# A two-layer model block with product-key experts: its second layer, second block and retrieval run for half the tokens at a time, and two token tiles are gathered instead of one

## The chip, the cores and the metric

The kernel runs on one core of a Trainium2 chip. The time is device microseconds (us) of one execution. A core has TensorE (PE, with its weight loads PEld), VectorE (DVE), ScalarE (ACT), GpSimd (POOL) and SyncE (SP), which issues most of the DMAs. All matrices are f32; a product of full accuracy is made either directly in f32, which the trace shows as two records per matmul, or in three passes of the rounded type fp32r.

## The reference

512 tokens of width 1024, with 16 meta tokens ahead of them, go through a first block of two layers, a second block, and a layer of product-key experts. Cut to what matters:

```python
for l in range(2):                                 # first block
    xn = _rmsnorm(h, pre_norm_g[l])
    proj = xn @ w_in[l] + b_in[l]                  # ten parts, 10240 columns
    y_a = _short_conv_branch(...)                  # looks back two tokens
    y_b = _retention_branch(...)                   # a token sees those before it
    y = (sigmoid(g_a) * y_a + sigmoid(g_b) * y_b) @ w_o[l]
    h = h + _rmsnorm(y, post_norm_g[l])
xn = rms_norm(h, norm1_g)                          # second block
h = h + concat(hgrn2(xn), gla(xn)) @ w_out         # two gated linear attentions, causal
hn = rms_norm(h, norm2_g)
q = (hn @ w_q).reshape(tokens, 8, 2, 128)          # retrieval: 8 heads, 2 x 128 sub-keys
s_top, i_top = top_k(q . sub_keys, 16)             # then the best 16 of the 256 sums
expert, g = ..., softmax(best)                     # 128 experts for each token, of 16384
act = gelu(einsum('td,thkd->thk', hn, u[expert]))
h = h + einsum('thk,thkd->td', g * act, v[expert])
return rms_norm(h, norm_f_g)
```

Every layer and the second block look back only: the first 256 tokens never need the last 256.

## The kernel before, in words

**Weights.** All weights, U and V among them, lie in one DRAM array `ws`, cut in pieces of 128 x 1024. The program is a list of tasks, each with the pieces that it uses. `Weights.run` goes through it: it loads pieces in pairs of 1 MB, issued by SP (`raw`); it splits a piece into `hi` (ScalarE, L143) and `lo` = raw - hi (VectorE, L151), two pieces ahead and at high priority; then it calls the task, which makes three passes (hi.hi, lo.hi, hi.lo; L386, L887, L1721, L1765). A task with `direct=True` takes the raw piece in f32 (L688, L1718).

**Tokens.** The moving operand holds tokens as columns. Layer 0 and layer 1 run for all tokens: each weight is used for a first part of 272 or 256 columns and a second of 256. The second block and the retrieval have the two halves as separate steps, whose order `PLAN` writes out (the first digit of a word is the half): FQ, KG, V and G are products with weights, S scores, M the mix, O the output, N the norm ahead of the retrieval, Q the retrieval's queries and keys.

**Background work.** Generators given to `W.later` or `bg` (norms, scores, `top_k`, the gate matrix) are advanced by `W.pace` steps per piece, from `PACE`; `W.flush` runs them out at once. A tile scheduler then sets each engine's order; every engine runs its instructions in that order.

**Experts.** Of four tiles of 128 tokens, the first three (`NDENSE`, ND = 384 columns) go through all 16384 experts densely: `gate_matrix` makes a dense matrix of the weights of the retrieved experts (L1438 and L1445 on VectorE, L1453 on TensorE) and puts it into DRAM as `gate_d`; `u_task` makes 128 experts' activations (the first `AHEAD` = 28 of the 128 groups direct, L1718, the rest L1721), `weigh` multiplies them by the gates (L1738) and splits them (`hw`, L203, L204), and `v_task` (L1765) sums V over them in PSUM. The fourth tile is gathered: for each of its 128 slots `fetch` brings one row of U and V for each token, 8 KB, by an indirect DMA that GpSimd issues (L1635) into one of four buffers; VectorE makes the dot product (L1671) and the weighted sum (L1663). The gather runs in the background of the dense stage, from expert group 6 on.

## Time and profile before

| what | value |
|---|---|
| median of 3 runs | 3297.1 us (3294.66 to 3298.0) |
| the profiled execution | 3293.4 us, its span 3291.6 |
| TensorE matmul, busy | 3250.3 us, 99% of the span |
| VectorE, busy | 2036.7 us, 62% |
| ScalarE, busy | 1302.2 us, 40% |
| GpSimd, busy | 186.3 us, 6% |
| DMA | 532 MB, mean 162 GB/s |

The span is the time from the first to the last instruction that the profiler recorded. Busy time is that of instructions on the engine; a wait isn't busy. The engines run beside each other, so the shares don't add up to one.

### The profile page before, as it was taken

The numbers are of one execution on the slowest core, as the hardware profiler recorded it, in microseconds if no ns is written. First come the engines' busy times: TensorE is split into PE (matmuls) and PEld (weight loads), VectorE is DVE, ScalarE is ACT, GpSimd is POOL, SyncE is SP. The second block draws the span as 40 slices with busy tenths as digits, with TensorE's granted clock in tenths as the row PEclk, the third lists the DMA queues.
The fourth block names the chain that finished last, engine by engine and source line by source line (L and its number), as shares of the span: only waits on it lengthen the run. The fifth ranks groups of instructions, "written<-read, shape, count | busy, mean of one in ns | idle before, by whom it ended". The sixth has DMA issues, their size and how long they took to land. (4 is left out here: it accounts for less than half of the span.)

```text
span 3291.6 us, 51099 instructions
## 1 busy us (share of the span) xinstructions
PE 3250.3 (99%) x21063; PEld 2974.2 (90%) x21063; DVE 2036.7 (62%) x4019; ACT 1302.2 (40%) x2388; POOL 186.3 (6%) x132
## 2 busy tenths in 40 slices
PE   8999999999999999999999999999999999999999
PEld 7999999999889999999998988766789999999998
DVE  6545554433744555443465659998898888888443
ACT  5343242323534324232455533356443333333333
POOL 0000000000000000000000000000132222222000
PEclk9999999999999999999999999999999999999999
DMA  6222222222422222222232123346899988998442
GB/s 216 75 86 88 77 78 90 90 90 103 176 75 99 87 84 78 90 90 100 106 129 90 52 91 140 129 181 239 305 373 346 345 333 314 351 356 325 143 147 95
DMA packets 129961, 532.04 MB, mean 162 GB/s; under 512 B 9136, under 2 KB 60992, under 8 KB 73280
## 3 DMA queue, kind: packets, MB, share of 16 engines
q1 hardware_dynamic: 103520, 368.19, 31.2%
q0 software_dynamic: 18432, 134.23, 10.6%
q10 hardware_dynamic: 7776, 26.37, 2.0%
q8 instruction: 165, 2.70, 0.3%
q14 instruction: 68, 0.56, 0.0%
HBM read 501.48 MB, written 27.26 MB: 161 GB/s over the span
## 5 line engine op out<-in xcount | busy, mean ns | idle before, releaser
L143 ACT ACTIVATE hi<-raw 128x1024 fp32r<-128x1024 f32 x532 | 563.4, 1060 | 1404.1 <-PE ps L386 626.7
L151 DVE TENSOR_TENSOR lo<-raw,hi 128x1024 fp32r<-128x1024 f32 x532 | 650.6, 1224 | 753.3 <-ACT hi L143 748.4
L386 PE MATMUL ps<-xnh,hi 128*128 128x256 f32 (+1 forms) x2464 | 513.7, 283 | 0.0
L386 PE MATMUL ps<-xnl,hi 128*128 128x256 f32 (+1 forms) x2464 | 513.5, 283 | 0.0
L386 PE MATMUL ps<-xnh,lo 128*128 128x256 f32 (+1 forms) x2464 | 512.9, 283 | 0.0
L1765 PE MATMUL ps<-hi,hw 128*128 128x512 f32 x1536 | 427.0, 393 | 3.3 <-ACT hid L1730 2.8
L1721 PE MATMUL ps<-hn,hi 128*128 128x384 f32 x1600 | 409.5, 337 | 0.0
L386 PEld LDWEIGHTS ps<-xnh,lo 128*128 128x128 f32 x2464 | 385.8, 189 | 0.0
L386 PEld LDWEIGHTS ps<-xnh,hi 128*128 128x128 f32 x2464 | 384.7, 188 | 1.1
L386 PEld LDWEIGHTS ps<-xnl,hi 128*128 128x128 f32 x2464 | 384.4, 188 | 0.1
L1635 POOL DMA_INDIRECT uv<-uv,idx x128 | 186.1, 1454 | 2843.8 <-PE ps L1650 2336.8
L1765 PEld LDWEIGHTS ps<-hi,hw 128*128 128x128 f32 x1536 | 287.7, 188 | 63.6 <-ACT hid L1730 3.5
L1721 PEld LDWEIGHTS ps<-hn,hi 128*128 128x128 f32 x1600 | 290.8, 188 | 4.3
L1721 PE MATMUL ps<-hn,lo 128*128 128x384 f32 x800 | 269.2, 337 | 0.0
L1765 PE MATMUL ps<-lo,hw 128*128 128x512 f32 x768 | 239.5, 392 | 0.0
L1765 PEld LDWEIGHTS ps<-lo,hw 128*128 128x128 f32 x768 | 144.7, 188 | 32.1
L1663 DVE SCALAR_TENSOR_TENSOR acc<-uv,dots,acc 128x1024 f32<-128x1024 f32 x127 | 163.0, 1284 | 3.2
L1671 DVE SCALAR_TENSOR_TENSOR uv<-uv,hnT 128x1024 f32<-128x1024 f32 x128 | 155.8, 1219 | 10.5 <-DMA uv<-uv,idx 10.4
L1718 PE MATMUL ps<-hn,raw 128*128 128x384 f32 x448 | 149.5, 490 | 5.0 <-ACT stage L1462 4.7
L1721 PEld LDWEIGHTS ps<-hn,lo 128*128 128x128 f32 x800 | 150.0, 188 | 0.1
L887 PE MATMUL ps<-x,hi 128*128 128x256 f32 x768 | 141.4, 288 | 4.0 <-ACT x L274 3.4
L1718 PEld LDWEIGHTS ps<-hn,raw 128*128 128x128 f32 x448 | 83.4, 190 | 62.6 <-ACT stage L1462 8.1
(353 smaller groups left out, 5103.6 us busy)
## 6 DMA issues: line engine op xcount, KB each, us to landing
raw<-ws SPq DMA_DIRECT2D x313, 1024.0 KB, 4.8
gate_d<-stage ACTq DMA_DIRECT2D x48, 512.0 KB, 3.4
gates<-gate_d SPq DMA_DIRECT2D x16, 1536.0 KB, 13.1
dm<-decay_m SPq DMA_DIRECT2D x8, 264.0 KB, 5.1
vb<-vbias SPq DMA_DIRECT2D x8, 256.0 KB, 6.3
dc<-decay SPq DMA_DIRECT2D x8, 256.0 KB, 5.6
uv<-uv,idx POOLq DMA_INDIRECT x128, 7.6
h<-ht SPq DMA_DIRECT2D x2, 544.0 KB, 4.4
```

Source lines behind the costliest of these rows:

```text
L143: nc.scalar.activation(hi, raw[i], AF.Copy)
L151: nc.vector.tensor_tensor(out=lo, in0=r, in1=parts[i][0].bitcast(F32), op=OP.subtract)
L386: nc.tensor.matmul(t[:, :b - a], w[wi][:, off + k, :], x[k].t[xi][:, a:b], start=(k == 0 and n == 0), stop=(k == K - 1 and n == 2))
L887: nc.tensor.matmul(p, parts[wi][:, k, :], x[k][:, xi], start=(k == 0 and n == 0), stop=(k == K - 1 and n == 2))
L1635: nc.gpsimd.indirect_dma_start(out=t, out_offset=None, in_=ins["uv"], in_offset=bass.IndirectOffsetOnAxis(ap=idx[i][:, j:j + 1], axis=0))
L1663: nc.vector.scalar_tensor_tensor(out=acc, in0=v, scalar=dots[:, j:j + 1], in1=acc, op0=OP.mult, op1=OP.add)
L1671: nc.vector.scalar_tensor_tensor(out=u, in0=u, scalar=1.0, in1=hnT, op0=OP.mult, op1=OP.mult, accum_out=dots[:, j:j + 1])
L1718: nc.tensor.matmul(ps, w[0][:, k, :], tl["hn32"][k][:, :ND], start=k == 0, stop=k == KD - 1)
L1721: nc.tensor.matmul(ps, w[wi][:, k, :], tl["hn"][k][:, xi], start=(k == 0 and n == 0), stop=(k == KD - 1 and n == 2))
L1765: mm = nc.tensor.matmul(tl["acc"][t][b], h[:, hi, t * 128:(t + 1) * 128], w[vi][:, b * 512:(b + 1) * 512], start=(e == 0 and n == 0), stop ...
```

## The change

Layer 0 stays as it was. What follows is done for the first 256 tokens (with the meta tokens) up to and including the retrieval's queries, then for the other 256: layer 1 (`late_layer`, called by `second_layer`), the second block by a shorter `PLAN`, the retrieval. All pieces of layer 1, the second block and the retrieval's queries are read, and where it applies split, once for each half. What the second half needs of the first (keys and values of both blocks) goes to DRAM and is read back (`left_kq`, `left_vm`, `left_vh`, `left_k`, `left_v`).

Tiles 0 and 1 are now gathered, tiles 2 and 3 dense (ND = 256, the first 32 groups of U direct). U and V rows are gathered apart, 256 rows of 4 KB for each token, into three buffers (`ROWS`). The generator of the gather has a queue of its own, `W.slow`, advanced by `pace2` steps per piece: 1.45 from the retrieval of tiles 0 and 1 on, 1.1 in the dense stage; `end_gathering` runs it out at expert group 124. From piece 128 on (layer 1 and everything behind it), `lo` of every second piece is made by GpSimd. The output projection of layer 1 and the second block's FQ are direct for both halves. Line numbers of the changed kernel: L812 and L806 are passes and direct products of layer 1, L1337 the second block's direct ones, L158 `lo`, L2085 the dot product, L2096 the weighted sum, L1871 and L1878 the gate matrix, L2141 the product with the gates, L211 the split's second part.

```diff
-NDENSE = 3
-ND = 128 * NDENSE
-NHN = 3
-AHEAD = 22 + 2 * NHN
-PACE = (3, 1, 2, 2, 2, 3.75, 6.5, 1.5, 1, 0.7)
+ND = HALF
+AHEAD = 32
+PACE = (3, 1, 2, 2, 2, 3.75, 6.5, 1.5)
+GATHER = (1.45, 1.1)
+ROWS = 3
+POOLED = 128
 SAFTER = 1
-QCUT = 15
 TICK2, TICKU = 4, 2
...
-PLAN = "FQ00 P3 S00 P4 FQ01 S01 !N1 KG V0 G0 FQ10 S02 V1 S10 M00 FQ11 S11 G1 S12 M01 M10 O0 P8 M11 N0 Q00 O1 Q01 N1 P5 Q1"
+PLAN = "FQ0 P3 S0 P4 FQ1 S1 KG S2 V0 G0 V1 F G1 M0 M1 O N Q"
...
         self.pump(int(self.credit))
         self.credit -= int(self.credit)
+        self.credit2 = min(self.credit2 + self.pace2 * share, 3)
+        while self.credit2 >= 1 and self.slow:
+            self.credit2 -= 1
+            if next(self.slow[0], self) is self:
+                self.slow.pop(0)
...
-                    nc.vector.tensor_tensor(out=lo, in0=r, in1=parts[i][0].bitcast(F32), op=OP.subtract)
+                    eng = nc.gpsimd if flat[i][0] >= POOLED and i % 2 else nc.vector
+                    eng.tensor_tensor(out=lo, in0=r, in1=parts[i][0].bitcast(F32), op=OP.subtract)
...
+                def wo_task(m):
+                    def f(w):
+                        if m % 2 == 0:
+                            st["y2", m // 2] = slot("y2", 2 * N).rearrange("p (a c) -> p a c", a=2)
+                        ps = proj(w, 0, N, x=[st["yb", k // 2][:, k % 2] for k in range(KD)])
+                        y = st["y2", m // 2][:, m % 2]
+                        nc.scalar.activation(y, ps, AF.Copy)
+                        st.setdefault("ss", Sum()).add(y)
+                    return f
...
+                def post_norm():
+                    r = rstd_of(slot("rstd", N), st["ss"].total())
+                    yield
+                    total = Sum()
+                    for m in range(KD):
+                        x = hs[m][:, q0:f1]
+                        y = st["y2", m // 2][:, m % 2]
+                        nc.vector.scalar_tensor_tensor(out=y, in0=y, scalar=col(C_POST + m), in1=r,
+                                                       op0=OP.mult, op1=OP.mult)
+                        nc.vector.tensor_tensor(out=x, in0=x, in1=y, op=OP.add)
+                        total.add(x)
...
+            def second_norms(half):
+                total = yield from late[half]["post_norm"]()
+                yield from halves[half]["norm1"](total)
...
+            def second_layer(half):
...
+                    for m in range(KD):
+                        add(L["wo_task"](m), direct=True)
...
+                do(W.flush)
+                if half == 0:
+                    do(phase, 1)
+                    bg(first_norms, 1)
+                do(setattr, W, "pace", PACE[0])
+                order(L, 1, add, qk, wo)
...
+                            W.add(H["pair_task"](which, 2 * a + c), N0 + 4 * a + 2 * k + c, direct=True)
...
+                    do(lambda: W.later(H["norm2"](), name="norm2", first=True))
                     do(W.flush, "norm2")
...
+                    do(H["load_keys"])
+                    if s == 0:
+                        do(lambda: W.later(first_block.late[1]["pre_norm"](rstd2[:, HALF:]), first=True))
+                    for c in range(16):
+                        W.add(H["wq_task"](c), N0 + 36 + c, direct=s == 1)
+                    do(H["keys"], 15)
+                    if s == 0:
+                        do(lambda: W.later(experts.begin(), name="top0"))
+            for s in range(2):
+                first_block.second_layer(s)
+                bg(first_block.second_norms, s)
+                do(W.flush)
+                for word in PLAN.split():
+                    if word[0] == "P":
+                        do(setattr, W, "pace", PACE[int(word[1:])])
+                    else:
+                        name = word.rstrip("01234")
+                        step(s, name, int(word[len(name):] or 0))
...
+        def begin():
+            gp = ctx.enter_context(tc.tile_pool(name="gather", bufs=1, side="right", reuse_waits="tile"))
+            W.slow.extend(gathered(i, gp) for i in range(2))
+            W.pace2 = GATHER[0]
+            yield
...
+            def row():
+                return p.tile([128, D], F32, tag="row", bufs=ROWS, name="row")
...
+                if j < 2 * NSLOT:
+                    t = rows[j] = row()
+                    table, j = ("pu", j) if j < NSLOT else ("pv", j - NSLOT)
...
+            dots = p.tile([128, NSLOT], F32, tag="dots", name="dots")
+            acc = p.tile([128, D], F32, tag="acc", name="acc")
+            for j in range(NSLOT):
+                u = rows.pop(j)
+                nc.vector.scalar_tensor_tensor(out=u, in0=u, scalar=1.0, in1=hnT, op0=OP.mult,
+                                               op1=OP.mult, accum_out=dots[:, j:j + 1])
+                fetch(j + ROWS)
+                yield
+            nc.scalar.activation(dots, dots, AF.Gelu)
+            nc.vector.tensor_tensor(out=dots, in0=dots, in1=gw[i], op=OP.mult)
+            for j in range(NSLOT):
+                v = rows.pop(NSLOT + j)
+                if j == 0:
+                    nc.vector.tensor_scalar(out=acc, in0=v, scalar1=dots[:, j:j + 1], scalar2=None, op0=OP.mult)
+                else:
+                    nc.vector.scalar_tensor_tensor(out=acc, in0=v, scalar=dots[:, j:j + 1], in1=acc,
+                                                   op0=OP.mult, op1=OP.add)
+                fetch(NSLOT + j + ROWS)
+                yield
...
+        def end_gathering():
+            for x in W.slow:
+                for _ in x:
+                    pass
+            W.slow.clear()
-        for e in (*range(18, AHEAD), *range(18)):
+        for e in range(AHEAD):
             if e == 8:
-                do(W.flush, "top")
+                do(W.flush, "top1")
...
+        do(setattr, W, "pace2", GATHER[1])
         for e in range(0, 128, 2):
-            if e == ENDS:
-                do(W.flush)
+            if e == 124:
+                do(end_gathering)
```

Where layer 1 ends and the second block begins, TensorE of the kernel before has (`yc` a branch of layer 1, `sg` the operand of its output projection, `sq` the squares of a norm, `nt` the normed tokens):

```order
L688 MATMUL ps<-sg,raw 128x256 x8
L247 MATMUL ps<-sq,mean 128x256
L688 MATMUL ps<-sg,raw 128x256 x32
L247 MATMUL ps<-sq,mean 128x256
L688 MATMUL ps<-sg,raw 128x256 x24
L883 MATMUL ps<-nt,raw 128x256 x15
L247 MATMUL ps<-sq,mean 128x256
L883 MATMUL ps<-nt,raw 128x256 x33
```

and the changed kernel, at the end of each half's layer 1 (L254 the norms' sums, L1680 the low gate):

```order
L812 MATMUL ps<-yc,hi 128x256 x2
L812 MATMUL ps<-yc,lo 128x256
L806 MATMUL ps<-yb,raw 128x256 x63
L254 MATMUL ps<-sq,mean 128x256 x2
L1337 MATMUL ps<-nt,raw 128x256 x6
L1680 MATMUL ps<-x,glp 16x256
L1337 MATMUL ps<-nt,raw 128x256 x40
```

Before, the norms' sums stood among the matmuls of the output projection and of FQ; now two stand together between them.

In the stage of the direct U, VectorE before has the gate matrix alone (`oh` the one-hot rows of 4 tokens):

```order
L1445 TENSOR_TENSOR oh<-oh,picks_102 128x1024 x2
L1438 TENSOR_TENSOR oh<-it_100,picks_102 128x1024 x2
L1445 TENSOR_TENSOR oh<-oh,picks_102 128x1024 x2
L1438 TENSOR_TENSOR oh<-it_100,picks_102 128x1024 x2
L1445 TENSOR_TENSOR oh<-oh,picks_102 128x1024 x2
```

and the changed kernel there:

```order
L1871 TENSOR_TENSOR oh<-it_97,picks_100 128x1024 x2
L1878 TENSOR_TENSOR oh<-oh,picks_100 128x1024 x2
L2085 SCALAR_TENSOR_TENSOR row,dots<-row,hnT 128x1024
L1871 TENSOR_TENSOR oh<-it_97,picks_100 128x1024 x2
L2085 SCALAR_TENSOR_TENSOR row,dots<-row,hnT 128x1024 x2
L1878 TENSOR_TENSOR oh<-oh,picks_100 128x1024 x2
L1871 TENSOR_TENSOR oh<-it_97,picks_100 128x1024 x2
L1878 TENSOR_TENSOR oh<-oh,picks_100 128x1024 x2
L1871 TENSOR_TENSOR oh<-it_97,picks_100 128x1024 x2
L2085 SCALAR_TENSOR_TENSOR row,dots<-row,hnT 128x1024
```

Dot products of gathered rows have moved in among the gate matrix.

At the end of the program VectorE before has the last products with the gates, the last splits, and the final norm (L1612, L1623):

```order
L1738 TENSOR_TENSOR hid<-hid,gates 128x384
L204 TENSOR_TENSOR hw<-hid,hw 128x384
L151 TENSOR_TENSOR lo<-raw,hi 128x1024
L204 TENSOR_TENSOR hw<-hid,hw 128x384
L1612 TENSOR_TENSOR r<-ss 128x1
L1623 SCALAR_TENSOR_TENSOR o<-ps,r,gf 128x512 x2
```

and the changed kernel (L2106 adds the residual to the gathered tile):

```order
L2096 SCALAR_TENSOR_TENSOR acc<-row,dots,acc 128x1024
L158 TENSOR_TENSOR lo<-raw,hi 128x1024
L2141 TENSOR_TENSOR early<-early,gates 128x256
L2096 SCALAR_TENSOR_TENSOR acc<-row,dots,acc 128x1024
L211 TENSOR_TENSOR hw<-early,hw 128x256
L2096 SCALAR_TENSOR_TENSOR acc<-row,dots,acc 128x1024 x35
L2106 TENSOR_TENSOR acc<-ps,acc 128x512 x2
```

Behind the last split now stand 35 weighted sums of the gather and the end of its tile.

## Rows read from the trace of the kernel before

**Rows 1.** The page, busy time, share of the span and instructions of each engine.

```profile
PE 3250.3 (99%) x21063; PEld 2974.2 (90%) x21063; DVE 2036.7 (62%) x4019; ACT 1302.2 (40%) x2388; POOL 186.3 (6%) x132
```

**Rows 2.** Windows by stage: us, busy of PE, PEld, DVE, ACT, POOL, PEclk, DMA, GB/s.

```profile
12.50:846.00 833.50, 833.50 (x6098) 798.39 (x6099) 410.47 (x678) 303.50 (x530) 0.00 (x0) 1.00 0.27 97
846.00:1660.00 814.00, 814.00 (x6026) 778.44 (x6025) 395.16 (x621) 296.62 (x507) 0.00 (x0) 1.00 0.28 98
1660.00:2113.00 453.00, 444.06 (x2945) 403.98 (x2944) 320.23 (x1114) 214.62 (x457) 0.00 (x0) 0.98 0.29 103
2113.00:2323.00 210.00, 197.55 (x1226) 131.17 (x1224) 181.69 (x553) 125.05 (x273) 0.00 (x0) 1.00 0.55 205
2323.00:3291.60 968.60, 958.63 (x4770) 861.14 (x4768) 724.30 (x1040) 357.35 (x613) 186.09 (x128) 1.00 0.77 286
```

**Rows 3.** Windows of one line's matmuls: L386, L688, L1721, L1765 (us, PE, PEld).

```profile
1500.00:1600.00 100.00, 100.00 (x848) 100.00 (x847) 1.00 0.27 96
...
1631.40:1660.00 28.60, 27.93 (x128) 24.24 (x128) 1.00 0.31 111
...
2323.00:3291.60 968.60, 429.03 (x2400) 421.98 (x2400) 1.00 0.77 286
...
2323.00:3291.60 968.60, 540.43 (x2304) 432.40 (x2304) 1.00 0.77 286
```

**Rows 4.** Groups of instructions: busy us, mean ns of one, idle before and its releaser.

```profile
L1453 PE MATMUL ps<-oh 128*128 128x128 f16 x768 | 51.4, 219 | 7.4 <-ACT stage L1462 5.6 <-DVE oh L1438 1.5 <-DVE oh L1445 0.3
...
L143 ACT ACTIVATE hi<-raw 128x1024 fp32r<-128x1024 f32 x532 | 563.4, 1060 | 1404.1 <-PE ps L386 626.7
...
L1671 DVE SCALAR_TENSOR_TENSOR uv<-uv,hnT 128x1024 f32<-128x1024 f32 x128 | 155.8, 1219 | 10.5 <-DMA uv<-uv,idx 10.4
...
L1671 DVE DVE_READ_ACCUMULATOR uv<-uv,hnT 128x1 f32 x128 | 10.6, 83 | 0.0
...
L1663 DVE SCALAR_TENSOR_TENSOR acc<-uv,dots,acc 128x1024 f32<-128x1024 f32 x127 | 163.0, 1284 | 3.2
...
L1438 DVE TENSOR_TENSOR oh<-it,picks 128x1024 f16<-128x1024 f16 x96 | 63.0, 686 | 22.4 <-PE ps L1453 22.1
L1445 DVE TENSOR_TENSOR oh<-oh,picks 128x1024 f16<-128x1024 f16 x96 | 61.9, 684 | 0.0
...
L204 DVE TENSOR_TENSOR hw<-hid,hw 128x384 fp32r<-128x384 f32 x128 | 70.7, 553 | 5.4 <-ACT hw L203 5.4
...
L151 DVE TENSOR_TENSOR lo<-raw,hi 128x1024 fp32r<-128x1024 f32 x532 | 650.6, 1224 | 753.3 <-ACT hi L143 748.4
```

**Rows 5.** Windows, a stretch of the dense stage; the last column is GB/s.

```profile
2340.00:2500.00 160.00, 159.52 (x738) 135.99 (x737) 141.45 (x209) 61.89 (x109) 47.44 (x31) 1.00 0.97 365
```

**Rows 6.** The window of both retrievals; a top-k step on VectorE there and up to 2323.

```profile
1958.00:2113.00 155.00, 150.67 (x906) 138.84 (x907) 139.55 (x758) 58.20 (x142) 0.00 (x0) 0.96 0.36 130
...
L1322 DVE MAX8 best<-cand 128x8 f32<-128x88 f32 x22 | 5.0, 246 | 0.0
...
L1322 DVE MAX8 best<-cand 128x8 f32<-128x88 f32 x10 | 2.0, 236 | 0.0
```

**Rows 7.** The window of the second block, both halves.

```profile
1660.00:1958.00 298.00, 293.38 (x2039) 265.14 (x2037) 180.68 (x357) 156.42 (x316) 0.00 (x0) 1.00 0.25 89
```

**Rows 8.** A group of the post-norm on VectorE.

```profile
L703 DVE SCALAR_TENSOR_TENSOR y<-y,cols,rstd 128x256 f32<-128x256 f32 (+1 forms) x32 | 13.2, 483 | 8.8 <-ACT rstd L249 8.8
```

**Rows 9.** Waits of TensorE: what for, us in total, times, longest.

```profile
PE ps L247 <- DVE sq L353: 8.3, 2, 7.2
...
PE ps L887 <- ACT x L274: 3.4, 1, 3.4
```

**Rows 10.** GpSimd's group; one record's min/median/max in ns; the gather's DMA to landing.

```profile
L1635 POOL DMA_INDIRECT uv<-uv,idx x128 | 186.1, 1454 | 2843.8 <-PE ps L1650 2336.8 <-DVE acc L1663 480.0 <-DVE acc L1661 15.1
...
L1635 POOL DMA_INDIRECT uv<-uv,idx x128: 939/1678/2752, 2337.3 to 3028.7; - x128
...
DMA to landing us min/median/max: 5.5/7.6/14.4
```

More of the change, by code (lines that the diff above doesn't have):

```diff
@@ L711, in first_block @@
                 layers.append(layer)
[L713 to L734 removed]
+            cols1 = []
@@ L799, in first_block @@
                         add(L["g_task"](m + 2, "b"))
-                    if m == KD - 3:
+                    if m == KD - 3 and l == 0:
                         do(L["halve_all"])
-                at = n[0]
-                if l == 1:
-                    do(lambda: second_block.tables())
-                for half in range(2):
-                    if half:
-                        if l == 0:
-                            do(layers[1]["setup"])
-                        do(setattr, W, "pace", PACE[2])
-                        bg(norm_between, l, 0)
-                    n[0] = at
-                    for m in range(KD):
-                        add(L["wo_task"](m, *OWN[l][half]), direct=half == 1)
@@ new lines, in first_layer, with add, qk, wo @@
+            def first_layer():
+                L = layers[0]
+                n = [0]
+                def add(f, **k):
+                    W.add(f, n[0], **k)
+                    n[0] += 1
+                def qk(h):
+                    for half in range(2) if h == 0 else [None]:
+                        if h == 0:
+                            n[0] = 0
+                        for hh in (0, 1) if h == 0 else [h]:
+                            for which in "qk":
+                                for part in range(2):
+                                    rng = FULL if half is None else [FULL[half]]
+                                    add(L["qk_task"](hh, which, part, rng),
+                                        direct=half == 0 and 4 * hh + 2 * "qk".index(which) + part < DIRECT[0])
+                        if half == 0:
+                            do(W.flush)
+                def wo():
+                    at = n[0]
+                    do(end_beside)
+                    do(late_setup)
+                    for half in range(2):
+                        if half:
+                            do(setattr, W, "pace", PACE[2])
+                            bg(first_norms, 0)
+                        n[0] = at
+                        for m in range(KD):
+                            add(L["wo_task"](m, *FULL[half]), direct=half == 1)
+                    assert n[0] == 128
+                do(L["setup"])
+                bg(L["pre_norm"], *FULL[0])
+                do(W.flush)
+                bg(L["pre_norm"], *FULL[1])
+                do(setattr, W, "pace", PACE[0])
+                order(L, 0, add, qk, wo)
@@ new lines, in second_layer, with add, qk, wo @@
+            def second_layer(half):
+                L = late[half]
+                n = [128]
+                def add(f, **k):
+                    W.add(f, n[0], **k)
+                    n[0] += 1
+                def qk(h):
+                    for hh in (0, 1) if h == 0 else [h]:
+                        for which in "qk":
+                            for part in range(2):
+                                add(L["qk_task"](hh, which, part),
+                                    direct=half == 0 and 4 * hh + 2 * "qk".index(which) + part < DIRECT[1])
+                def wo():
+                    do(second_block.tables if half == 0 else (lambda: None))
+                    for m in range(KD):
+                        add(L["wo_task"](m), direct=True)
+                    assert n[0] == 256
+                do(W.flush)
+                if half == 0:
+                    do(phase, 1)
+                    bg(first_norms, 1)
+                do(setattr, W, "pace", PACE[0])
+                order(L, 1, add, qk, wo)
@@ L1757, in f @@
                 prev = None
[L1758 removed]
+                for t in range(2):
                     one = [(e, h, w) for e, h, w in zip(es, hw, ws)]
```

785 lines of the change are left out of this document (504 added, 281 removed).

## The prediction

> **What bounds the kernel now.** I read the page's busy times first, then the span cut into stages, then the groups of the stages that change, then the waits of TensorE. The matmul engine is busy for 99% of the span [rows 1]: time is saved where its work shrinks, and lost where the change makes it wait. The sum is made against the profiled execution, 3293.4 us (the span of 3291.6 and 1.8 around it), which lies 3.7 under the median of the runs shown, 3297.1. A change of under 0.2%, some 7 us, can't be told from none.
>
> The stages [rows 2] are, in turn: layer 0, layer 1, second block with both retrievals, gate matrix with the direct part of U, dense experts. In each of them TensorE is busy for 94 to 100% of the time. The other columns show who has room. VectorE is busy half the time in the layers, 71% in the third, 87% in the fourth (181.7 of 210.0), 75% in the fifth. In the fifth the DMA engines run at 286 GB/s, and GpSimd does nothing but issue the gather.
>
> **What TensorE no longer does.** A matmul takes its time by its columns [rows 3]: with 256 columns 100.0/848 = 0.118 us in three passes, and 27.93/128 = 0.218 for one of the two records of a direct one; with 384 columns 429.0/2400 = 0.179 in passes; V's with 512 columns 540.4/2304 = 0.235.
> - Dense stage. U goes to 96 experts x 24 = 2304 matmuls of 256 columns, 272 us; V to 128 x 12 = 1536, 360 us. With 10 for the residual and the end it is 642 in place of 968.6: **-327**.
> - Direct U: 32 experts x 16 records x 0.218 = 112. The gate matrix took 51.4 [rows 4] for three tiles, so 34 for two. Together 146 in place of 210.0: **-64**.
> - Direct in place of three passes, in the output projection of the first half and in the second block's FQ of the second half: 64 matmuls each at 2 x 0.218 - 3 x 0.118 = 0.08: **+10**.
> - Layer 1 and the rest of the second block have the same columns in all, in matmuls of one half at a time; no row says that a half costs more.
>
> TensorE's own sum becomes 3293 - 327 - 64 + 10 = 2912.
>
> **What the other engines must now hide.** All of layer 1 is read and split once per half. ScalarE's split takes 1.06 [rows 4]: 128 more are 136 us, and it was busy for 297 of 814 [rows 2]. The reads double from 98 GB/s, and the gather comes on top; the dense stage moved 365 GB/s over 160 us without a gap on TensorE [rows 5]. So both are hidden, at nothing; without that cover the reads would bind first.
>
> VectorE is the one that runs short. A gathered row costs it 1.219 + 0.083 for the dot product and 1.284 for the weighted sum [rows 4], 2.59 in all, for 256 rows 662 us in place of 331. That work leaves the dense stage, where it was covered, and is laid from layer 1 of the second half on. From the instruction order of the changed kernel, by stage: 102 dot products in layer 1 of the second half, 76 weighted sums and dots in its second block, about 60 dots and 41 sums in its retrieval and direct-U stage, and 196 rows in the dense stage, the last 35 of them behind every other instruction of the experts. Every second subtraction `lo` of these stages goes to GpSimd.
> - Retrieval of the second half and direct U. The four tiles' top-k lie in the two windows of [rows 6] (22 + 10 = 32 of the second step, eight heads a tile). VectorE's time there, 139.6 + 181.7 [rows 2, 6], less the gate matrix of 63.0 + 61.9 [rows 4], is 196, at most 49 a tile; subtractions, norms and additions lie there as well, and I take 43. Two tiles: 85. Gates for two tiles: 83. Gathered rows 60 x 1.30 + 41 x 1.28 = 131. With 6 for splits: 305 us. TensorE has 112 + 34 and 16 direct query pieces of 16 records (56) with some 14 of keys, 216. **+89**, between 0, if the scheduler's priorities let the rows slip further, and 131, if none is covered.
> - Second block of the second half: VectorE had 180.7 us for two halves [rows 7], so 90 for one, and 76 rows at 1.30 are 99: 189 against TensorE's 298/2 = 149. **+40** (0 to 99).
> - Top-k of tiles 0 and 1 was run beside the second retrieval, where TensorE was busy for 150.7 of 155 us [rows 6]. Now it runs at the start of the second half's layer 1, in the first 28 pieces: their passes last 28 x 24 x 0.118 = 79 us, while VectorE has 85 for top-k, 14 subtractions (17) and some 28 of norm and rotary work, 130. I take **+45** (0 to 51).
> - Norms. The changed code flushes the post-norm and the next norm of each half with nothing beside them. For the first half: eight scalings and additions of the layer's output (at most 0.483 each [rows 8]), 7.7, eight scalings for the next norm, 3.9, and the sum of squares with its root between them; where such a sum was waited for, it was 7.2 at once [rows 9]. **+20** (10 to 30); the second half's is inside the +40. The norm ahead of each retrieval: **+16**, eight per half (4 to 10).
> - Seams: each of the eight head and block steps has half the columns to hide the same chain of evictions, and a wait at such a place was 3.4 [rows 9]: **+20** (0 to 27).
> - Rest of layer 1, second half: 102 dots (133) and 125 of VectorE's own are 258, against 316 of TensorE: hidden. Dense stage: 68 dots, 128 sums (253, of which 45 stand in the tail), 112 subtractions at 1.22, `hw` at two thirds of 0.553 and the product with the gates, of the same size, alike, 94: 484 against 642. Hidden, as long as VectorE isn't held up.
> - Tail: 35 weighted sums behind the last expert. At VectorE's own pace 1.28 each, 45 us. With three row buffers, each must land (5.5 at least), be used (1.28) and be asked for (1.45) [rows 4, 10]: 8.2/3 = 2.7, so 96 us. Less the 8 that the end takes anyway, 37 to 88: **+62**, the middle.
>
> Sum: 2912 + 89 + 40 + 45 + 20 + 16 + 20 + 62 = 3204; with the 3.7 of the median 3208, so 3210.
>
> **A price that no row shows.** GpSimd did no arithmetic before. From the second half's layer 1 on it has some 182 subtractions (60 in the layer, 10 in the block, 112 dense). The nearest rows are VectorE's own subtraction, 1.22, and GpSimd's slowest record, 2.75 [rows 4, 10]. If it works beside VectorE, either fits: 112 x 2.75 = 308 and 128 row issues (186) against 642. That is what I took: nothing. No row of before has the two at work on operands of this size.
>
> The Trainium skill, page "SBUF — State Buffer", section "Who interferes with whom", says that a VectorE instruction with two SBUF inputs contends with a GpSimd instruction that reads SBUF. By that page the subtraction on GpSimd would not be free here, since `lo`, the dots and the sums all have two such inputs; if the two shut each other out, the sum would be that of the first rival. No run of before shows it. The Trainium skill's page "GPSIMD Engine Reference", section 3.1, states 4497 ns for 2048 elements on GpSimd against 2293 on VectorE; by it, my estimate for 1024 elements would be 2.25 us, and the first rival would give 3403.
>
> **The rivals.**
> - *GpSimd's subtraction and VectorE take turns* (slower). Then each subtraction's price p is added to VectorE's sums: dense 484 + 112p against 642, binding from p = 1.4; layer 1 of the second half 258 + 60p against 316, from 0.97; the block +10p. At 1.22: 15 + 12 = +27, 3235. At 2.75: 150 + 107 + 28 = +285, 3495. It decides against the change from p = 1.7 on: 32 + 44 + 17 = +93, 3303. Partly shared, it lies between: I give this case 3240 to 3440. For it: all of VectorE's heavy rows here read two SBUF tiles. Against it: nothing that rows show.
> - *The overloads hide* (faster). The rows are handed out by credit and can slip to the dense stage, which has 158 us to spare, and top-k lies behind the matmuls as it did [rows 6]. Then only norms, seams and tail are left: 2912 + 56 + 62, and a part of the 174: 2990 to 3100. Against it: the order already shows where VectorE stands between the rows.
> - *The three-buffer loop sets the pace*. With the median landing of 7.6 [rows 10] a row takes (7.6 + 1.3 + 1.45)/3 = 3.45 us, and 512 rows 1766 us. They start with the second half's layer 1, at about 846 + 407 + 226 + 85 = 1564, and would end at 3330. For it: the loop was waited for in before too, 480 of GpSimd's idle time. Against it: rows now are half as long, and the shortest landing gives 2.7 and an end well ahead of this.
> - *The change does nothing*: that the matmuls of a half cost as much as the whole's. 0.118 at 256 columns against 0.179 at 384 is in proportion [rows 3]; I give it no chance of its own.
>
> **How the numbers follow.** Forecast, 3120 to 3270: 45%. Taking turns, 3240 to 3440: 30%. Hidden, 2990 to 3100: 15%. Loop, 3270 to 3340: 10%. Faster: 45 + 15, 7 of the 30 and 2 of the 10, 69%. Within 0.2%: 4 and 2, 6%. Slower: 19 and 6, 25%. The range 3040 to 3380 leaves out about half of the hidden case and a third of the first rival, under 2 in 10; the likeliest case's own is 3120 to 3270.
>
> **What would show it.** Right: the dense stage near 640 us, with TensorE busy; direct U and gates longer than its matmuls, and waiting for VectorE; some 35 weighted sums at the end behind the last matmul of V. Wrong: TensorE waiting for `lo` of GpSimd, or VectorE's dots and sums longer than 1.22 and 1.28 while GpSimd works (first rival); VectorE idle, waiting for a row's DMA, from the second half on (loop); TensorE 99% busy in every stage (hidden). The largest doubt in the forecast itself is how VectorE's queue shares its time between splits and rows, 174 us of the sum.

## The result, and the profile after

The changed kernel takes 3542.1 us (median of 4 runs, 3537.5 to 3548.5) against 3295.9 for the kernel before: the ratio is 1.0749, with a 95% interval of 1.0727 to 1.0771. The forecast was 3210, with a range up to 3380: the sign, the size and the range were missed.

The page's busy times of the changed kernel answer to [rows 1]:

```profile
span 3536.5 us, 51255 instructions
...
PE 3030.7 (86%) x19948; PEld 2755.9 (78%) x19948; DVE 2530.7 (72%) x4271; ACT 1374.6 (39%) x2388; POOL 1298.3 (37%) x835
```

TensorE's work did shrink, from 3250 to 3031 us, but it is now idle for 506 us. Windows by stage (columns as in [rows 2]): layer 0; layer 1 of the first half; its second block and retrieval; layer 1 of the second half; its second block; its retrieval with the direct U; the dense stage; the tail:

```profile
12.50:844.00 831.50, 831.28 (x6095) 796.62 (x6096) 410.97 (x679) 304.55 (x536) 0.00 (x0) 1.00 0.27 97
844.00:1265.00 421.00, 411.80 (x2930) 389.93 (x2930) 215.04 (x378) 208.12 (x336) 149.61 (x84) 0.98 0.52 183
1265.00:1540.00 275.00, 235.69 (x1526) 211.49 (x1524) 173.51 (x484) 131.79 (x255) 57.32 (x27) 0.92 0.36 126
1540.00:2086.00 546.00, 433.67 (x3046) 405.83 (x3046) 486.48 (x922) 216.28 (x357) 323.94 (x215) 0.90 0.74 261
2086.00:2362.00 276.00, 205.75 (x1104) 177.99 (x1104) 208.54 (x268) 92.31 (x175) 128.45 (x99) 0.80 0.73 248
2362.00:2739.00 377.00, 242.70 (x1366) 205.43 (x1366) 314.92 (x919) 110.38 (x259) 115.61 (x108) 0.81 0.80 273
2739.00:3452.00 713.00, 667.22 (x3880) 567.58 (x3880) 668.94 (x556) 301.65 (x447) 493.29 (x270) 0.99 0.86 297
3452.00:3536.50 84.50, 0.00 (x0) 0.00 (x0) 47.66 (x57) 4.52 (x16) 29.92 (x29) 0.53 0.66 211
```

Every stage from the second half on is longer than forecast: 546 for 452, 276 for 189, 377 for 305, 713 for 642, 84 for 70. VectorE is busy for 94% of the dense stage. In the two stages where TensorE waits for the largest share of the time its granted clock is 0.80 and 0.81, part of the time on its lower level: the second block's 1104 matmul records are busy for 206 us where half of [rows 7], 1020 records, is 147. No term of the forecast had that.

Groups of the changed kernel on VectorE and GpSimd (busy us, mean ns), which answer to [rows 4]:

```profile
L158 POOL TENSOR_TENSOR lo<-raw,hi 128x1024 fp32r<-128x1024 f32 x256 | 644.2, 2517 | 1367.8 <-ACT hi L149 1324.2
...
L158 DVE TENSOR_TENSOR lo<-raw,hi 128x1024 fp32r<-128x1024 f32 x388 | 508.5, 1311 | 367.2 <-ACT hi L149 364.2
...
L2085 DVE SCALAR_TENSOR_TENSOR row<-row,hnT 128x1024 f32<-128x1024 f32 x256 | 394.7, 1549 | 66.4 <-DMA row<-pu,idx 66.0
L2096 DVE SCALAR_TENSOR_TENSOR acc<-row,dots,acc 128x1024 f32<-128x1024 f32 x254 | 382.2, 1505 | 108.4 <-DMA row<-pv,idx 106.9
L211 DVE TENSOR_TENSOR hw<-early,hw 128x256 fp32r<-128x256 f32 x128 | 170.4, 1340 | 26.6 <-ACT hw L210 25.8 <-issue 0.5
```

Dots and sums went from 1.22 and 1.28 to 1.55 and 1.51, and `hw`, a third narrower than before, from 0.55 to 1.34. How, the timeline of the dense stage shows (start, us, engine): VectorE first, then GpSimd in the same stretch.

```profile
2905.98 3.09 DVE L211 TENSOR_TENSOR hw<-early,hw 128x256 fp32r<-128x256 f32 x1 [0.48 <-ACT hw L210]
2909.00 1.21 DVE L2085 SCALAR_TENSOR_TENSOR row<-row,hnT 128x1024 f32<-128x1024 f32 x1
...
2911.61 4.10 DVE L2085 SCALAR_TENSOR_TENSOR row<-row,hnT 128x1024 f32<-128x1024 f32 x1
...
2919.21 2.71 DVE L211 TENSOR_TENSOR hw<-early,hw 128x256 fp32r<-128x256 f32 x1 [0.48 <-ACT hw L210]
```

```profile
2906.39 2.40 POOL L158 TENSOR_TENSOR lo<-raw,hi 128x1024 fp32r<-128x1024 f32 x1
...
2912.20 2.41 POOL L158 TENSOR_TENSOR lo<-raw,hi 128x1024 fp32r<-128x1024 f32 x1
...
2919.22 2.41 POOL L158 TENSOR_TENSOR lo<-raw,hi 128x1024 fp32r<-128x1024 f32 x1
```

Each long VectorE instruction lies over a subtraction on GpSimd. The last `hw` starts with it, at 2919.21, and ends 0.29 us after it: next to nothing of its 0.42 us was done while GpSimd subtracted. A dot beside no subtraction takes 1.21. Counted over the whole trace: of the 510 dots and sums the 411 beside no subtraction take 1.29 at most, and of the 99 beside one 63 take over 1.5, up to 4.11. That points to the operands in SBUF: an addition that reads one operand from PSUM (L1039, `yb<-ps,yb`) takes 0.41 in the median with a subtraction beside it (23 times) and without (25 times).

The waits of VectorE and of TensorE (us in total, times, longest):

```profile
DVE acc L2096 <- DMA row<-pv,idx: 106.9, 89, 5.3
DVE row L2085 <- DMA row<-pu,idx: 66.0, 43, 4.0
```

```profile
PE ps L2078 <- DVE hn L2075: 74.0, 3, 54.2
PE ps L254 <- DVE sq L240: 50.1, 7, 21.3
PE ps L1886 <- DVE oh L1878: 36.7, 22, 7.2
PE ps L1845 <- DVE f L1798: 33.4, 1, 33.4
PE ps L1603 <- DVE on L1591: 26.8, 5, 12.5
PE ps L1845 <- DVE ex L1818: 21.4, 1, 21.4
```

VectorE stands for 173 us behind rows that have not come. Everything that TensorE waits for longest is VectorE's: the top-k (L1798, L1818) and what is queued behind it, norms (L240), gate matrix (L1878). For GpSimd's `lo` it waits 21 us in all, so that GpSimd's own slowness is not where the time goes.

### The profile page after: what moved, and what is told of

Read it like the earlier page. It is cut to its first block, busy times and chain, and to the rows that moved or that the text cites. A ratio compares the mean times of both kernels' runs of the same rounds, so it can differ in the third digit from the quotient of the medians.

```text
span 3536.5 us, 51255 instructions
## 1 busy us (share of the span) xinstructions
PE 3030.7 (86%) x19948; PEld 2755.9 (78%) x19948; DVE 2530.7 (72%) x4271; ACT 1374.6 (39%) x2388; POOL 1298.3 (37%) x835
## 4 chain that ended last, share of the span: by engine, by line
DVE 13%; PE 11%; issue 11%; DMA 10%; POOL 7%; ACT 2%; POOLq 0%; DVEq 0%; ACTq 0%
DMA row<-pv,idx 7%; POOL row L2064 4%; PE ps L812 3%; POOL lo L158 3%; PE ps L2164 3%; DVE acc L2096 3%; DMA row<-pu,idx 3%; DVE lo L158 2%; PE ps L2130 2%; DVE row L2085 2%; PE ps L2127 1%; DVE early L2141 1%; ACT hi L149 1%; DMA raw<-ws 1%; PE ps L993 0%
## 5 line engine op out<-in xcount | busy, mean ns | idle before, releaser
L158 POOL TENSOR_TENSOR lo<-raw,hi 128x1024 fp32r<-128x1024 f32 x256 | 644.2, 2517 | 1367.8 <-ACT hi L149 1324.2
L158 DVE TENSOR_TENSOR lo<-raw,hi 128x1024 fp32r<-128x1024 f32 x388 | 508.5, 1311 | 367.2 <-ACT hi L149 364.2
L2064 POOL DMA_INDIRECT row<-pu,idx x256 | 312.7, 1222 | 446.4 <-DVE row L2085 302.1
L2096 DVE SCALAR_TENSOR_TENSOR acc<-row,dots,acc 128x1024 f32<-128x1024 f32 x254 | 382.2, 1505 | 108.4 <-DMA row<-pv,idx 106.9
L812 PE MATMUL ps<-xn,hi 128*128 128x256 f32 (+1 forms) x2432 | 448.0, 286 | 7.3 <-DVE P L211 2.6
L2064 POOL DMA_INDIRECT row<-pv,idx x256 | 306.7, 1198 | 383.5 <-DVE acc L2096 274.3
L2085 DVE SCALAR_TENSOR_TENSOR row<-row,hnT 128x1024 f32<-128x1024 f32 x256 | 394.7, 1549 | 66.4 <-DMA row<-pu,idx 66.0
L812 PEld LDWEIGHTS ps<-xn,hi 128*128 128x128 f32 x2432 | 382.0, 192 | 9.9 <-issue 4.0
L812 PE MATMUL ps<-xn,lo 128*128 128x256 f32 (+1 forms) x1216 | 346.2, 285 | 8.6 <-DVE lo L158 4.5
L2130 PE MATMUL ps<-hn,hi 128*128 128x256 f32 x1536 | 278.1, 281 | 0.0
L435 PE MATMUL ps<-xnh,hi 128*128 128x272 f32 (+1 forms) x1248 | 263.6, 284 | 0.0
L812 PEld LDWEIGHTS ps<-xn,lo 128*128 128x128 f32 x1216 | 233.3, 192 | 11.5 <-DVE lo L158 5.8
```

What stands on the lines that cost most here:

```text
L158: eng.tensor_tensor(out=lo, in0=r, in1=parts[i][0].bitcast(F32), op=OP.subtract)
L435: nc.tensor.matmul(t[:, :b - a], w[wi][:, off + k, :], x[k].t[xi][:, a:b], start=(k == 0 and n == 0), stop=(k == K - 1 and n == 2))
L812: nc.tensor.matmul(p, w[wi][:, off + k, :], x[k].t[xi][:, a:b], start=(k == 0 and n == 0), stop=(k == K - 1 and n == 2))
L2064: nc.gpsimd.indirect_dma_start(out=t, out_offset=None, in_=ins[table], in_offset=bass.IndirectOffsetOnAxis(ap=idx[i][:, j:j + 1], axis=0))
L2085: nc.vector.scalar_tensor_tensor(out=u, in0=u, scalar=1.0, in1=hnT, op0=OP.mult, op1=OP.mult, accum_out=dots[:, j:j + 1])
L2096: nc.vector.scalar_tensor_tensor(out=acc, in0=v, scalar=dots[:, j:j + 1], in1=acc, op0=OP.mult, op1=OP.add)
```

## The experiments

Theory 1 is the first rival: VectorE's instructions with two SBUF operands and GpSimd's subtraction take turns. Theory 2, its opponent: VectorE is overbooked anyway, and GpSimd relieves it. Theory 3: rows come late, and VectorE's queue stands behind them. Theory 4: the rows' work itself is too much from the second half on. Times are medians; the kernel before ran at 3293.5 to 3294.3 beside them.

### Where `lo` is made

**e1_lo_on_vector**

```diff
-POOLED = 128
+POOLED = 10 ** 9
```

> The changed kernel with every `lo` on VectorE, none on GpSimd (POOLED out of reach). Theory 1, taking turns: a VectorE instruction that reads two SBUF tiles waits while GpSimd subtracts, up to the 2.5 us of one subtraction. Then the dots and sums fall from 1.55 and 1.51 to 1.22 and 1.28 in the mean, with none over 1.5, `hw` from 1.34 to about 0.37, and the time falls by 200 to 300 us, to 3240 to 3340, although VectorE makes 256 subtractions more (313 us). Theory 2, VectorE is overbooked by the gathered rows in stages without room, and GpSimd's subtractions relieve it: the dots stay long, and the time rises above 3542, to 3600 or more.

Measured: 3442.7 us, ratio 1.0444 (1.0417 to 1.0470); 100 us less than the changed kernel, with 256 subtractions more on VectorE, which is nevertheless busy for 2392 us in place of 2531. No dot is over 1.27 us (min/median/max in the view of the row tiles), and `hw` is back at 0.42:

```profile
L2085 DVE SCALAR_TENSOR_TENSOR row<-row,hnT x256: 1170/1218/1274, 1591.3 to 2967.4; 128x1024 f32<-128x1024 f32 x128
...
L2096 DVE SCALAR_TENSOR_TENSOR acc<-row,dots,acc x254: 1247/1283/1323, 2023.5 to 3427.2; 128x1024 f32<-128x1024 f32 x127
```

Theory 2 is out. But theory 1 had foreseen 3240 to 3340: the 100 to 200 us that are missing are not GpSimd's.

**e2_gpsimd_first_half**

```diff
+        alone = [i for i, x in enumerate(flat) if x[0] == 128][1]
...
-                    eng = nc.gpsimd if flat[i][0] >= POOLED and i % 2 else nc.vector
+                    eng = nc.gpsimd if flat[i][0] >= POOLED and i % 2 and i < alone else nc.vector
```

> The changed kernel with GpSimd's subtractions only in the first half's layer 1 and second block, where no row is gathered; from the second half's layer 1 on all `lo` on VectorE. Theory 1: the second half, the direct U and the dense stage go as with every `lo` on VectorE, and the first half stays as it is in the changed kernel (421 + 275 us); the whole is within 40 us of the run with all on VectorE, above rather than below. Theory 2: the time lies above 3542, since the relief is missing where VectorE has most to do.

Measured: 3433.8, ratio 1.0429 (1.0411 to 1.0448), 9 us under e1. GpSimd's subtractions cost nothing in the first half, where VectorE has room; the 100 us arise from the second half on.

**e3_before_gpsimd** (the kernel before)

```diff
-                    nc.vector.tensor_tensor(out=lo, in0=r, in1=parts[i][0].bitcast(F32), op=OP.subtract)
+                    eng = nc.gpsimd if i % 2 else nc.vector
+                    eng.tensor_tensor(out=lo, in0=r, in1=parts[i][0].bitcast(F32), op=OP.subtract)
```

> The kernel before with every second `lo` on GpSimd, nothing else: 266 of 532 subtractions. Theory 1: VectorE's dots and sums in the dense stage, 1.22 and 1.28, get longer in the mean by 0.2 or more, the longest near 4 us; VectorE has idle time there (724 busy of 969), so the whole is 0 to 40 us longer. Theory 2: dots and sums keep their 1.22 and 1.28, and the time is the same or a little shorter.

Measured: 3308.0, ratio 1.0045 (1.0028 to 1.0061). The kernel before gets the same long instructions, the dots in the mean 1.44:

```profile
L1672 DVE SCALAR_TENSOR_TENSOR uv<-uv,hnT x128: 1208/1218/3961, 2357.1 to 3062.2; 128x1024 f32<-128x1024 f32 x128
```

So the stretching belongs to the pair of engines, not to the new order; with VectorE idle for a quarter of the stage it shows as 0.45%.

### What the rows cost

**e4_few_rows** and **e8_few_rows_lo_on_vector**

```diff
-                if j < 2 * NSLOT:
+                if j < 2 * NROW:
...
-            for j in range(NSLOT):
+            for j in range(NROW):
```

with NROW = 4; the second also has `POOLED = 10 ** 9`.

> The changed kernel with 4 of the 128 slots of each gathered tile: 124 are left out, with their DMAs, dots and sums. GpSimd's subtractions stay. Theory 1: `hw` stays well above its 0.37 (now 1.34) and layer 1 of the first half keeps its 421 us, since neither depends on the gather; the whole falls to 3080 to 3200. Theory 2: VectorE has room everywhere, `hw` is 0.4, and the whole falls to TensorE's own sum with the bare norms, 2970 to 3060.

> 4 of the 128 slots of each gathered tile, as in the run with few rows (124 are left out), and every `lo` on VectorE. What is left is the halving itself. Theory 1 (taking turns): 20 to 70 us under the 3116 of the run with few rows, 3045 to 3095, with `hw` at 0.37. If the halving's own waits (norms, top-k, seams) hold TensorE and not VectorE's stretched instructions, it stays within 15 us of 3116.

Measured: 3115.7 (0.9458, 0.9442 to 0.9474) and 3110.6 (0.9446, 0.9430 to 0.9462). Without rows, GpSimd's turns cost 5 us, no more than the spread of one kernel's runs (3108.8 to 3115.7), although `hw` still takes 1.35 with them: VectorE has time to wait. Here the second expectation of theory 1 (20 to 70 us) fell. And the halving, with the two dense tiles and almost no gather, takes 3111.

**e7_rows_stay** and **e15_rows_stay_gpsimd** (the second with `POOLED = 128`)

```diff
-                if j < 2 * NSLOT:
+                if ROWS <= j < 2 * NSLOT:
+                    rows[j] = rows["all"][j % ROWS]
+                elif j < 2 * NSLOT:
                     t = rows[j] = row()
+                    rows.setdefault("all", []).append(t)
...
-                nc.vector.scalar_tensor_tensor(out=u, in0=u, scalar=1.0, in1=hnT, op0=OP.mult,
+                nc.vector.scalar_tensor_tensor(out=acc, in0=u, scalar=1.0, in1=hnT, op0=OP.mult,
```

> Every `lo` on VectorE; of each gathered tile only the first three rows are brought, and all dots and sums work on these (the other rows' DMAs are left out; a dot writes its product into the tile of the sums, so that the row stays). VectorE's work is the same, no row is ever late. Theory 3: the waits for rows are gone, the tail is gone, 3220 to 3320. Theory 4: 3400 or more, since VectorE's load is what counts.

> The rows stay (three rows of each tile are brought, the others' DMAs are left out), and every second `lo` from piece 128 on by GpSimd again. GpSimd now does nothing but subtract, and no row is late. Taking turns: 60 to 160 us over the 3213 of the same with all `lo` on VectorE, dots and sums above 1.45 in the mean. If GpSimd's subtraction cost only by holding back the row DMAs behind it: 3213 or less.

Measured: 3212.9 (0.9749, 0.9733 to 0.9765) and 3418.7 (1.0382, 1.0365 to 1.0399). With all of VectorE's work and all but six row DMAs left out, the kernel is 230 us under e1, 7 below what theory 3 had foreseen, and 2.5% under the kernel before: theory 4 as the sole cause is out. The run takes away late rows and the rows' traffic at once and can't tell one from the other. With GpSimd's subtractions on top it loses 206 us, more than the 60 to 160 foreseen; no row DMA is there to be held back behind the first six, so the price is VectorE's stretched instructions. Its sums, its dots (L2099 and L2088 in this kernel) and what TensorE waits for longest:

```profile
L2099 DVE SCALAR_TENSOR_TENSOR acc<-row,dots,acc 128x1024 f32<-128x1024 f32 x254 | 413.0, 1626 | 1.9
L2088 DVE SCALAR_TENSOR_TENSOR acc<-row,hnT 128x1024 f32<-128x1024 f32 x256 | 361.4, 1412 | 5.0 <-DMA row<-pu,idx 3.5
...
PE ps L2167 <- DVE lo L158: 64.7, 31, 3.9
```

In all TensorE waits 122 us for the `lo` that VectorE still makes (2.9 in e7) and 2.1 for GpSimd's: the subtractions that stayed on VectorE come late behind the stretched instructions.

**e5_four_rows** and its control **e6_two_lo_control**; **e9_five_rows**; **e10_six_rows**

```diff
-ROWS = 3
+ROWS = 4
...
-SPLITS_AHEAD, SUBS_AHEAD = 2, 2
+SPLITS_AHEAD, SUBS_AHEAD = 2, 1
```

with all `lo` on VectorE; the control leaves ROWS at 3. Five rows put `acc` into the place of hnT (`tag="hnT"`); six also have SPLITS_AHEAD = 1.

> Every `lo` on VectorE, and four row buffers in place of three; the room is taken from `lo` (SUBS_AHEAD 1, two buffers), as in the next run, which is its control. Theory 3, late rows: three buffers can't bring rows as fast as VectorE would use them, VectorE stands 166 us behind the rows' DMA in the run with all `lo` on VectorE, and all that is queued behind it is late too. Then the waits for rows fall to under 90 us, the weighted sums behind the last expert vanish, and the time falls by 80 to 160 us against the control, to 3280 to 3370. Theory 4, load: VectorE simply has more work from the second half on (1538 us of it, against some 1414 of TensorE's); then the time stays within 30 us of the control.

> Control for four rows: every `lo` on VectorE, three row buffers, two buffers for `lo` in place of three. Both theories: within 30 us of the 3443 of the run with every `lo` on VectorE, rather above it.

> Every `lo` on VectorE, two `lo` buffers, five row buffers: the tile of the sums takes the place of hnT once the dots are done. Late rows: three buffers 3446, four 3369, rows that are never late 3213; with five the waits for rows (95 us with four) fall to 30 to 60, and the time to 3270 to 3330. If the load counts, it stays within 25 us of the 3369 of four rows.

> As with five rows, and a sixth buffer in place of the third `hi` (SPLITS_AHEAD 1). Late rows: 20 to 60 us under five rows, 3230 to 3290, unless a `hi` that comes later takes it back; then TensorE shows new waits for `hi` or `lo` in layer 0, whose 831 us would grow.

Measured: 3369.3 (1.0223, 1.0206 to 1.0240), control 3446.0 (1.0470, 1.0452 to 1.0487), five 3361.5 (1.0204, 1.0187 to 1.0221), six 3398.6 (1.0312, 1.0295 to 1.0329). The fourth buffer takes away 77 us, the tail among them, and VectorE's waits for rows fall from 199 to 94 us; the fifth takes away only 8, though these waits fall to 50. So five rows missed the 3270 to 3330 of late rows and came out as the load's expectation had it: late rows alone are not what separates 3361 from 3213. The sixth buffer missed its 3230 to 3290 as well. It was paid for with a `hi` buffer: TensorE waits for `hi` for 31 us in the dense stage (11 with five rows), VectorE 531 in all (25 with five), and the run tells nothing of rows.

**e13_rows_unused** (from five rows)

```diff
-                nc.vector.scalar_tensor_tensor(out=u, in0=u, scalar=1.0, in1=hnT, op0=OP.mult,
-                                               op1=OP.mult, accum_out=dots[:, j:j + 1])
+                nc.vector.tensor_copy(dots[:, j:j + 1], u[:, 0:1])
...
-                    nc.vector.scalar_tensor_tensor(out=acc, in0=v, scalar=dots[:, j:j + 1], in1=acc,
-                                                   op0=OP.mult, op1=OP.add)
+                    nc.vector.scalar_tensor_tensor(out=acc[:, :16], in0=v[:, :16], scalar=dots[:, j:j + 1],
+                                                   in1=acc[:, :16], op0=OP.mult, op1=OP.add)
```

> Five row buffers, every `lo` on VectorE, all 512 row DMAs, but of each row VectorE reads only the first column or the first 16 columns: the dots and sums are left out. Baseline is the run with few rows, 3111. If the rows' traffic holds the weights or the chains back, 3180 to 3260, with a dense stage above its 634 and weights that TensorE waits for; if only VectorE's time for the rows counts, 3105 to 3135.

Measured: 3201.9 (0.9717, 0.9701 to 0.9734): bringing the rows costs 91 us over 3111, though next to nothing is computed from them. The dense windows of the run with few rows and of this one:

```profile
2469.00:3102.00 633.00, 632.89 (x3871) 562.18 (x3869) 346.54 (x445) 302.34 (x452) 0.00 (x0) 1.00 0.58 202
```

```profile
2539.00:3205.00 666.00, 645.61 (x3879) 567.89 (x3877) 387.15 (x662) 305.63 (x459) 209.76 (x174) 0.98 0.89 335
```

Where rows are brought, the DMA engines are full (their packets take 99% of the time at 376 GB/s from 2700 to 3000), and a pair of weight pieces lands later. From issue to landing of `raw` between 2560 and 3000, with few rows (e8) and with five row buffers (e9):

```profile
DMA to landing us min/median/max: 4.6/4.8/6.9
```

```profile
DMA to landing us min/median/max: 5.7/8.6/15.4
```

In the kernel before the median was 7.2 there, and TensorE lost nothing; but from 2700 to 3000 it issued 36 pairs at 335 GB/s, e13 50. In the dense stage of e13 VectorE waits for no row, while TensorE waits 20 us for `hi`: these 33 us are the traffic's. The rest is lost in the second half's block and in the direct-U stage (28 and 45 us in the table below). There VectorE also stands for 103 us behind rows that have not come, so that traffic and late rows are not told apart.

**e14_rows_later** (from five rows)

```diff
-GATHER = (1.45, 1.1)
+GATHER = (1.0, 1.5)
```

> Five rows, with the pace of the gather 1.0 and 1.5 in place of 1.45 and 1.1 steps per piece: fewer rows in the second half's layer 1 and the direct-U stage, where VectorE is full, more in the dense stage; in the instruction order 64 weighted sums then stand behind the last expert (82 us). If the placement of the rows is what is left of the loss: the second half's layer 1 falls from 577 by 30 to 70 us and direct U from 354 by 10 to 40, and with the tail the whole is 3330 to 3390. If the rows' traffic is: these stages stay within 15 us, and the tail makes it 3420 to 3450.

Measured: 3383.0 (1.0267, 1.0242 to 1.0293). The retrieval and direct-U stage, with no row in it, takes 248 us in place of 354, as it does without rows at all (250); but layer 1 of the second half stays at 582, and the tail is 116. The gain of one stage was handed to the end. This agrees with neither expectation whole: direct U was held by the rows, and the work that was put off came back at the end. Of layer 1 the run tells nothing: it holds 128 dots and 57 sums in both runs, so the slower pace took no row out of it.

### Two more

**e11_five_rows_gpsimd** (five rows with `POOLED = 128`)

> Five rows, and every second `lo` from piece 128 on by GpSimd again, as in the changed kernel. Taking turns: 60 to 140 us over five rows with all `lo` on VectorE, dots and sums in the mean above 1.4, since rows that come in time leave VectorE nearer to its limit. If the 100 us between the changed kernel and the run with every `lo` on VectorE came from the row DMAs that GpSimd issues late, behind its subtractions, and not from VectorE's stretched instructions: within 30 us of five rows, since five buffers hide a late issue.

Measured: 3453.6 (1.0486, 1.0468 to 1.0503), 92 us over five rows: theory 1 again, with dots at 1.42. Row DMAs that GpSimd issues late, the rival, would have cost under 30.

**e12_early_transposes** (from five rows; hnT of the first tile made ahead of the top-k)

```diff
+        def ready():
...
+            tl["gather"] = [gathered(i, gp) for i in range(2)]
+            next(tl["gather"][0])
+            next(tl["gather"][0])
```

> Five rows, and the normed tokens of the first gathered tile are made and turned ahead of the retrieval's top-k, not behind it. In all runs so far TensorE stood 56 to 58 us (54 in the changed kernel) in its queue ahead of these transposes, while VectorE did the top-k in front of their operands. If this wait is on the path: 30 to 58 us under five rows. If VectorE's top-k holds the next matmuls anyway: within 12 us of five rows.

Measured: 3364.2 (1.0208, 1.0191 to 1.0225), within its noise of five rows. The wait of 56 us for `hn` is gone, and in its place TensorE waits 41.5 us at once for `q`, a little further on in the same layer; at the second half's top-k (L1845) it waits 72.5 us in place of 57.2. A wait that a view names is the first in the queue and need not be the cause. That VectorE's top-k is the cause here is argued: it fills VectorE's queue in that stretch, and no run took it out.

## Why the prediction was wrong

Stages of some runs in us, from the matmuls that open and close them (the first wait of a stage counts to it, so the edges differ from the windows above, by up to 23 us):

| run | layer 1, first half | block, retrieval | layer 1, second half | its block | retrieval, U | dense | tail |
|---|---|---|---|---|---|---|---|
| changed kernel | 441 | 249 | 541 | 299 | 375 | 713 | 85 |
| e1: `lo` on VectorE | 439 | 246 | 571 | 296 | 327 | 644 | 86 |
| e9: five rows | 441 | 240 | 577 | 244 | 354 | 665 | 6 |
| e7: rows stay | 439 | 246 | 510 | 244 | 297 | 636 | 6 |
| e13: rows unused | 442 | 241 | 489 | 239 | 295 | 666 | 6 |
| e8: few rows | 439 | 246 | 489 | 211 | 250 | 633 | 7 |

- **TensorE's own work: right.** With few rows TensorE is busy for 2926 us; the sum said 2912, some 20 of which were waits of the kernel before. The dense stage takes 633 to 636 us where it isn't disturbed; the sum said 642.
- **GpSimd's subtraction at nothing: wrong.** This is one of the three steps that failed. It measured 100 us in the kernel as it is, and 206 where the rows are at hand. The first rival had the mechanism: with the measured median of 2.41 us a subtraction its formula gives 112 + 87 + 24 over 3210, 3433, and e15 took 3419; by stage e15 is 113 us over e7 in the dense stage (749 for 636), 84 in layer 1 (594 for 510) and 2 in the block. That it comes so near is partly luck: the formula has VectorE full in the dense stage, and it is busy for 670 of the 749. I had given it 30% for want of a row, and its range ended at 3440 since I added it to a forecast that lacked the next point. The Trainium skill, page "SBUF — State Buffer", section "Who interferes with whom", stated this contention of two-input VectorE instructions with a GpSimd that reads; the trace agrees, 2.71 us for a `hw` of 0.42. The Trainium skill's page "GPSIMD Engine Reference", section 3.1, led to an estimate of 2.25 us a subtraction; 2.41 was measured.
- **"Hidden, at nothing", of the reads and the gather: wrong.** This is the second step. The row that I took as cover, 365 GB/s without a gap [rows 5], was of a stage whose matmuls had 384 columns. Now each pair of pieces is used up faster, the rows come over a longer time, and bringing them costs 91 us (e13): 33 in the dense stage by the traffic alone, the rest together with rows that come late.
- **Rows in time: wrong.** This is the third step. I let the three-buffer loop set the tail only. The changed kernel's 512 rows span from 1589 to 3521 us, 3.77 each, where the third rival had 3.45 and an end at 3330; what it missed is that VectorE, in order, stands in front of a row that isn't there, with the norms and top-k that TensorE needs behind it. The fourth buffer was worth 77 us.
- **VectorE's load of rows: the place right in the main, the size high.** 89 + 40 were taken for direct U and the block, nothing for layer 1; rows that stay cost 102 over few rows, 47 and 33 there and 21 in layer 1. The tail of 62 is no load: it is gone where the rows stay, and with three buffers the end takes 85 us where the sum had 70.
- **The halving's own waits: too small.** Norms, top-k and seams were priced at 36 + 45 + 20 = 101. From 2912 to 3111 (less the 4 of the median) it is 195. The wait of 58 us ahead of the transposes, behind the top-k of the first half, is alone over the 51 that were the most for it. Some of the 195 is the granted clock: with few rows it is 0.92, 0.93 and 0.95 in layer 1, block and retrieval of the second half, and the block's 1110 matmul records are busy for 187 us where half of [rows 7] is 147.

So that the run without GpSimd's turns and without late rows takes 3213, beside the forecast's 3210, is partly chance: the halving was under-priced by some 94 us, the rows' load and the tail over-priced by 89. What took the kernel from there to 3542 is measured: three buffers and the transfers together 230 us, GpSimd 100.

**What stays open.** Rows' work (102) and rows' transfers (91) over few rows would make 3304; together, with five buffers, they took 3361. That the last 57 us are late rows in a full VectorE queue is argued from its waits (50 us with five rows), not shown. None of the runs that compute everything beats the kernel before.

## What to carry to other kernels

When work is moved to an idle engine, ask which operands it reads and who else reads from the same memory at that time; where no row shows the pair at work, a short run of the kernel before with just that edit (e3 took one line) tells the mechanism in advance. Its price depends on how full the other engine is: 14.5 us in e3, 5 without rows, 100 in the changed kernel, 206 in e15. Work that was free because a stage had slack is not free elsewhere: VectorE's rows and the transfers had been covered by the long dense stage, which the change shortened, and the top-k by the second retrieval. An engine's queue is in order, so a late transfer costs not its own wait but that of all that stands behind it; counting buffers against issue, landing and use is a sum of one line and belongs in every gather.

## What the runs showed of the hardware

- A VectorE instruction with two SBUF operands and a GpSimd subtraction largely shut each other out. In the changed kernel 37 of the 43 dots and sums that started behind a subtraction took 3.42 us in the median. Of the 56 that started ahead of one, 31 kept their time and 25 were stretched all the same, to 4.08 in the median while the subtraction kept its 2.41; 4.10 for a dot of 1.21 is half a microsecond more than both together. In e15 70 of the 72 that started first kept their time, and there the subtraction took 3.10 in the median. What decides between the two is not shown.
- A GpSimd subtraction of 128 x 1024 f32 takes 2.41 us in the median (1.97 times VectorE's 1.224).
- Indirect row DMAs beside weight loads: at 374 GB/s (e9) 1 MB of weights landed 8.6 us after its issue, at 207 GB/s without rows (e8) 4.8, both in the median; in the kernel before 7.2 at 335.
- TensorE's granted clock is lower in the stages with long waits: 0.80 in the second half's block and 0.81 in the stage behind it, where the changed kernel's TensorE waits for the largest share of the time, and 0.90 to 1.00 in its other stages with matmuls.
